# Moving the start addresses of the matmul operands in the MLP of a hybrid encoder block

## The chip, the core and the metric

The kernel runs on one core of a Trainium2 chip. The metric is device time in microseconds (us) for one execution. In the profile PE is the engine that multiplies matrices and PEld is its weight load; DVE, ACT and POOL are the vector, scalar and GpSimd engines, and SP issues most of the DMA transfers.

## The reference, cut to what matters

One layer (SEQ = 512 tokens, D_MODEL = 1024, D_FF = 2816) is attention in three head groups with an output projection, then a gated MLP with a causal convolution of width 3, then a gated per-layer input. The change touches the storage of the MLP's operands and of all weights that are split in two:

```python
def conv_gated_mlp(h, w_up, conv_w, conv_b, w_down):
    u = h @ w_up
    ...
    gate, val = jnp.split(c, 2, axis=-1)
    return (jax.nn.silu(gate) * val) @ w_down
...
h = h + conv_gated_mlp(rms_norm(h, ln_ffn[i]), w_up[i], conv_w[i], conv_b[i], w_down[i])
gate = jax.nn.sigmoid(rms_norm(h, ln_ple[i]) @ w_ple_gate[i])
h = h + (p[i] @ w_ple_proj[i]) * gate
```

## The kernel before

Every operand of a product is held as two float32r tiles, a high part and a low part: ACT copies the value into the high tile, DVE subtracts the high part from the value and writes the low tile (`split`, L207). Each product of two such operands is three matmuls (`mm3`, L223), and a matmul here always loads 128x128 stationary values (an LDWEIGHTS in the profile) and streams a moving operand of 256, 384 or 512 columns past them.

The parts that matter are these.

- **Wide products of the MLP** (`up_plain`, L1232, tile `u` in the profile): the stationary operand is a 128x128 part of a weight tile (`w_hi`, `w_lo`), the moving operand is one row block of the normed activations, `Th` or `Tl`, 512 columns. They are 960 matmuls.
- **Narrow products of the MLP**, 256 columns. One group is the up-projection by seven products in place of eight (`up_seven`, tiles `sX`, `sY`, `sZ`), whose moving operand is half a row block of `Th`/`Tl`, or a block of the sums `xh`/`xl`. The other is the down-projection, also by seven products (`Down.product`, tiles `dn_X`, `dn_Y`, `dn_Z`), whose moving operand is a block of a left tile (`g_ah`, `g_al`; for the last phase `xh`, `xl`). They are 1092 matmuls: 924 in the down-projection and 168 in the up-projection. `part` (L1089) cuts a weight tile into its 128-column parts.
- **Gate of the per-layer input** (tile `pg`): moving `Th`/`Tl`, stationary for the first four output blocks a weight tile (`w_hi`, `w_lo`), for the last four a left tile (`wg_ah`, `wg_al`, or the rest of `xh`, `xl`). The last block is done in two halves of 256 columns. **Projection of the per-layer input** (tile `pp`): moving a left tile (`pT_ah`, `pT_al`), 512 columns.
- **Projections of the attention** (`A_z`, `B_z`, `C_z` and their variants): here the activations `Th`/`Tl` are stationary and the split weights move. In the output projection (`wo`) the weights are stationary again.

All split weights go through one ring of tiles with the tags `whi` and `wlo`, 8 buffers each. The order of the MLP's work is set by a planner at the end of the function, which uses fixed costs per kind of work (a matmul group costs `n * 0.1177` us, L1043) and knows nothing of addresses; SP, POOL and the other engines get the order that it writes out. POOL adds weights in DRAM by accumulating transfers, one at a time (`add_sums`, L1168).

**Where the operands start.** What a matmul reads is a stretch of every one of 128 partitions, so an operand has one start address in bytes. Taken modulo 512, the program's allocation gives before the change:

- `Th`, `Tl`: 128. Every block starts at a multiple of 1024 bytes further on.
- weight tiles (`w_hi`, `w_lo`, 768 floats = 3072 bytes = 6 x 512): 128, and every 128-column part (512 bytes) the same.
- left tiles (`g_ah`, `g_al`, `pT_ah`, `wg_ah`, 7168 bytes = 14 x 512) and `xh`, `xl`: 320, and every block of 1024 bytes the same.

Below a pair such as (320, 128) means: moving operand at 320, stationary operand at 128, both modulo 512.

Of the kernel before, what the change touches and what calls it, by code (L numbers as in the profile page):

```python
# [8 lines left out]
F32 = mybir.dt.float32  # L9
F32R = mybir.dt.float32r  # L10
# [5 lines left out]
P = 128  # L16
D = 1024
S = 512
# [60 lines left out]
def kernel(ctx: ExitStack, tc: tile.TileContext, x, xt0, xt, pt_in, small, bias_c,  # L79
# [9 lines left out]
    nc = tc.nc  # L89
# [56 lines left out]


    pi = ctx.enter_context(tc.tile_pool(name="pi", bufs=1))
    W = {"pool": pi, "n": 768, "raw": 4, "hi": 8, "lo": 8}

    def load_w(src_fn, nk, m, n, name, eng=dve, gain=None, later=False):

        wp, we = W["pool"], W["n"]
        raw = wp.tile([P, we], F32, tag="wraw", bufs=W["raw"], name=f"{name}_r")
        for dst, src in src_fn(raw):
            dma = sp.dma_start(out=dst, in_=src)
            if later:
                tc.keep_in_program_order(dma)
        hi = wp.tile([P, we], F32R, tag="whi", bufs=W["hi"], name=f"{name}_h")
        lo = wp.tile([P, we], F32R, tag="wlo", bufs=W["lo"], name=f"{name}_l")  # L160
        hv, lv = (t[:, : nk * n].rearrange("p (k c) -> p k c", k=nk) for t in (hi, lo))
        rv = raw[:, : nk * m].rearrange("p (k c) -> p k c", k=nk)
        if later:
            def split():
                act.copy(hv[:, :, :m], rv)
                eng.tensor_tensor(out=lv[:, :, :m], in0=rv, in1=f32(hv[:, :, :m]), op=ALU.subtract)
                return hv, lv

            return split
        if eng == "dma":  # L170

            act.copy(hv[:, :, :m], rv)
            act.activation(lv[:, :, :m], rv, AF.Copy, scale=-1.0)
            nc.gpsimd.dma_start(out=lv[:, :, :m], in_=rv, accum_op=ALU.add)
            return hv, lv
        if gain is not None and eng is nc.gpsimd:
            for k in range(nk):
                eng.tensor_scalar(rv[:, k], rv[:, k], gain[:, k : k + 1], 1.0, ALU.mult, ALU.mult)
        if gain is None or eng is nc.gpsimd:
            act.copy(hv[:, :, :m], rv)  # L180
            eng.tensor_tensor(out=lv[:, :, :m], in0=rv, in1=f32(hv[:, :, :m]), op=ALU.subtract)
        else:
            for k in range(nk):
                hk, lk, rk = (v[:, k, :m] for v in (hv, lv, rv))
                act.activation(hk, rk, AF.Copy, scale=gain[:, k : k + 1])
                dve.scalar_tensor_tensor(lk, rk, gain[:, k : k + 1], f32(hk), ALU.mult, ALU.subtract)
        return hv, lv


    NRAW, NHI = 6, 7  # L190
    RING = {"raw": [], "hi": [], "lo": []}

    def in_turn(what, n):
        ring = RING[what]
        if len(ring) < n:
            tag = what
            if what == "raw" and len(ring) >= W["raw"]:
                tag = ("hi", "lo")[(len(ring) - W["raw"]) % 2]
            ring.append(pi.tile([P, 768], F32 if what == "raw" else F32R, tag=f"w{tag}", bufs=W[tag], name=f"w_{what}{len(ring)}"))
        else:  # L200
            ring.append(ring[-n])
        return ring[-1]
# [1 line left out]
    def raw_tile():  # L204
        return in_turn("raw", NRAW)

    def split(t, n, gain=None, to=None, eng=dve):  # L207

        hi, lo = to or [in_turn(q, NHI)[:, :n] for q in ("hi", "lo")]
        if gain is None:  # L210
            act.copy(hi, t[:, :n])
            eng.tensor_tensor(out=lo, in0=t[:, :n], in1=f32(hi), op=ALU.subtract)
        else:
            act.activation(hi, t[:, :n], AF.Copy, scale=gain)
            dve.scalar_tensor_tensor(lo, t[:, :n], gain, f32(hi), ALU.mult, ALU.subtract)
        return hi, lo
# [95 lines left out]
    def first_products():  # L312
        for k in range(KD):
            n = 384
            if k % 2 == 0:
                wh, wl = (pi.tile([P, 768], F32R, tag=f"w{q}", bufs=W[q], name=f"A0_{k // 2}_{q}") for q in ("hi", "lo"))
            a = slice((k % 2) * n, (k % 2 + 1) * n)
            th, tl = Th[k // 4][:, k % 4, :], Tl[k // 4][:, k % 4, :]
            g = h[:, 3, 0:1] if k == 0 else col(C_MIX, k)
            if k == 0:  # L320
                for c in (slice(0, H), slice(H, S)):
                    dve.tensor_scalar(th[:, c], XB[k][:, c], g, 1.0, ALU.mult, ALU.mult)
            elif k == 3:
                dve.tensor_scalar(th, XB[k], g, 1.0, ALU.mult, ALU.mult)
            else:
                act.activation(th, XB[k], AF.Copy, scale=g)
            act.copy(wh[:, a], WA[k])
            dve.tensor_tensor(out=wl[:, a], in0=WA[k], in1=f32(wh[:, a]), op=ALU.subtract)
            dve.scalar_tensor_tensor(tl, XB[k], g, f32(th), ALU.mult, ALU.subtract)
            for i, (ta, w) in enumerate(((Th, wh), (Th, wl), (Tl, wh))):  # L330
                for t in range(NT):
                    pe.matmul(z0[t][:, :n], tcol(ta, k, t), w[:, a], start=k == 0 and i == 0, stop=k == KD - 1 and i == 2)
            if k == 1:
                load_x(3)
        ws = [w() for w in first_b]
        for t in range(NT):
            stats(t)
        ev = [in_unit("A0", 0, 384, t, None, []) for t in range(NT)]

        rs = [ev[t][0](rest=False) for t in range(2)]  # L340
        for t in range(NT):
            ev[t][1](rs[t])
            if t < 2:
                rs.append(ev[t + 2][0](rest=False))
        for t in range(NT):
            ev[t][0](sums=False)
        return ws
# [723 lines left out]
                self.tiles = [q.rearrange("p j c -> p (j c)") for q in left_tiles(self.name)]  # L1071
            return [q[:, i * S : i * S + n] for q in self.tiles]

    def split_of(w, deps=(), gain=None, group=None, i=0):

        w.hi_slot = Slot("hi") if group is None else group.slot
        makes = [w.hi_slot] if not w.hi_slot.users else []

        def do():
            w.hi, w.lo = split(w.t, w.n, gain, None if group is None else group.get(i, w.n))  # L1080

        w.split = Task("do", [AC(w.n), DV(w.n * (1 if gain is None else 1.12))], do, (w.load, *deps), makes, [w.raw] + ([] if makes else [w.hi_slot]))
        return w
# [20 lines left out]
    def seven_weights(f):  # L1104

        size = (768, 768, 768, 768, 512)
        usum = USUM[f].rearrange("p i c -> p (i c)")
        ws = [tile_of(n, f"ws{f}_{i}", w_up[f][:, 768 * i : 768 * i + n] if i < 2 else usum[:, 768 * (i - 2) : 768 * (i - 2) + n],
                      deps=SUM_TASKS.get(("u", f), ()) if i > 1 else ()) for i, n in enumerate(size)]
        for w in ws:  # L1110
            split_of(w)
        order = (0, 1, 4, 3, 6, 5, 2)
        at_ = lambda j, i: part(ws[(4 * order[j] + i) // 6], (4 * order[j] + i) % 6)
        need_ = lambda j: [ws[q] for q in sorted({(4 * order[j] + i) // 6 for i in range(4)})]
        return at_, need_

    def down_weights(ph, n, name, tag="raw"):

        m = w_down[ph].shape[4]
        src = {f"{c + 1}{'eo'[i]}": w_down[ph][n, i, c] for i in range(2) for c in range(2)}  # L1120
        src.update({what: DSUM[ph][:, i, n] for i, what in enumerate(("S2", "S1", "1e2e", "1oS2"))})
        return lambda what: split_of(tile_of(m, f"{name}_{what}", src[what], tag, SUM_TASKS.get(("d", ph), ()) if "S" in what or "2e" in what else ()))

    def row_weights(src, name, gain=None, group=None, i=0):
        return split_of(tile_of(S, name, src), LAST_X if isinstance(group, Rest) else (), gain, group, i)
# [417 lines left out]
    def square3(j):  # L1543

        s = Slot("conv")
        sq_slots.append(s)
        first = j == 0

        def do():
            if first:  # L1550
                pin = mp.tile([P, D + 40], F32, tag="pin", bufs=1, name="sums3")
                v3["sums"], v3["rb"] = pin[:, :S], pin[:, S:D]
            v3[j] = v3["sums"] if first else mtmp(F32, 1, f"n3_sq{j}")
            act.activation(v3[j], hj(j), AF.Square)

        def add():
            (dve if j >= 6 else pool).tensor_tensor(out=v3["sums"], in0=v3["sums"], in1=v3[j], op=ALU.add)

        deps = [H_ADDS[j // 4, q] for q, p in PRODUCTS.items() if p[4] == j // 2 % 2]
        if first:  # L1560
            v3["last"] = Task("do", [AC(S)], do, deps, [sum_slot])
        else:
            a = Task("do", [AC(S)], do, deps, [s])
            v3["last"] = Task("do", [DV(S) if j >= 6 else ("pool", 1.35)], add, [a, v3["last"]], (), [s, sum_slot])
# [94 lines left out]
    t = 0.0  # L1659
# [122 lines left out]
```

## Time and profile before

| what | value |
|---|---|
| runs before | 708.51 us median of 3 (707.37 to 709.40) |
| the profiled execution, its own time | 709.23 us |
| its span, first to last instruction | 707.5 us |
| granted TensorE clock, mean | 0.999 |
| PE busy in the span | 691.2 us (98%) |
| DVE / ACT / POOL busy | 546.5 / 393.9 / 224.3 us |

Reading it: matmuls on PE are pipelined, and the profile gives each a duration from its start until its result is out. The 280 ns of a matmul with 256 columns and the 389 ns of one with 512 are such durations, and neighbours overlap. What a matmul costs in a stretch without idle time is the distance from its start to the next one's start. The chain of waits gives this directly, since it counts each piece only up to the start of the next: a piece "2.12 PE dn_X x18" is 18 matmuls at 117.8 ns.

### The profile page before, as it was taken

The page shows a single profiled execution, that of the slowest core. Times are in us where ns is not written, and L with a number is a line of the kernel's source. Part 1 is how long each engine was busy: PE and PEld are TensorE (multiplying, and loading weights), DVE is VectorE, ACT ScalarE, POOL GpSimd, SP SyncE. Part 2 cuts the span into 40 slices and gives each one's busy share as a digit, 9 for nine tenths or more (in the row PEclk, how much of TensorE's full clock was granted, in tenths as well). Part 3 has the DMA queues.
Part 4 walks back from the last instruction along what each step waited for, and adds up shares of the span by engine and source line. Part 5 has one row for each costly group of instructions (what it writes and reads, how often), then busy time and mean ns, then how long its engine had stood idle before and what let it go on. Part 6 is the DMA issues. An engine that isn't in the chain of part 4 may idle for free.

```text
span 707.5 us, 11539 instructions
## 1 busy us (share of the span) xinstructions
PE 691.2 (98%) x4028; PEld 618.6 (87%) x4028; DVE 546.5 (77%) x1110; ACT 393.9 (56%) x737; POOL 224.3 (32%) x324
## 2 busy tenths in 40 slices
PE   9988999999999999999999999999999999999997
PEld 8988989988999988868888899988988888999786
DVE  7678787887878874788877874798776787788764
ACT  6646766766666762566454543554444555546831
POOL 5676776757665440420111011001101110001310
PEclk9999999999999999999999999999999999999999
DMA  9454658746335313453686887878887774652531
GB/s 328 179 149 118 195 176 231 222 148 209 98 119 180 124 41 119 139 183 111 167 184 127 229 200 186 187 144 233 234 201 148 146 201 109 216 171 81 175 112 68
DMA packets 48471, 116.52 MB, mean 165 GB/s; under 512 B 5494, under 2 KB 7158, under 8 KB 48412
## 3 DMA queue, kind: packets, MB, share of 16 engines
q1 hardware_dynamic: 40476, 96.59, 42.0%
q0 software_dynamic: 7648, 18.88, 16.9%
q8 instruction: 32, 0.52, 0.3%
q10 hardware_dynamic: 288, 0.30, 0.1%
q14 instruction: 27, 0.22, 0.1%
HBM read 108.53 MB, written 31.47 MB: 198 GB/s over the span
## 4 chain that ended last, share of the span: by engine, by line
PE 78%; DVE 7%; DMA 6%; ACT 4%; POOL 2%; issue 2%; SPq 0%; ACTq 0%; POOLq 0%; DVEq 0%
PE u L105 30%; PE dn_X L105 9%; PE C_z L105 6%; PE pg L105 6%; PE wo L105 5%; PE dn_Y L105 4%; PE B_z L105 4%; PE dn_Z L105 2%; DMA bias_B<-fk_d 1%; DMA h<-in_x_dram 1%; PE sX L105 1%; DMA waq<-in_w_in_dram 1%; PE C_s L105 1%; PE C_po L105 1%; PE B_s L105 1%
## 5 line engine op out<-in xcount | busy, mean ns | idle before, releaser
L105 PE MATMUL u<-Tl,w_hi 128*128 128x512 f32 x320 | 124.9, 390 | 0.4 <-DVE Tl L105 0.4
L105 PE MATMUL u<-Th,w_hi 128*128 128x512 f32 x320 | 124.6, 389 | 0.0
L105 PE MATMUL u<-Th,w_lo 128*128 128x512 f32 x320 | 124.6, 389 | 0.0
L105 ACT CAST w_hi<-w_raw 128x768 fp32r<-128x768 f32 (+1 forms) x116 | 88.3, 784 | 62.1 <-PE dn_X L105 20.3
L105 DVE TENSOR_TENSOR w_lo<-w_raw,w_hi 128x768 fp32r<-128x768 f32 (+1 forms) x114 | 101.4, 909 | 17.4 <-ACT w_hi L105 16.5
L105 DVE SCALAR_TENSOR_TENSOR c<-u,cols,c 128x511 f32<-128x511 f32 x80 | 59.5, 746 | 22.2 <-ACT c L105 21.1
L105 PEld LDWEIGHTS u<-Tl,w_hi 128*128 128x128 f32 x320 | 60.1, 188 | 13.3 <-DVE Tl L105 1.3
L105 PEld LDWEIGHTS u<-Th,w_lo 128*128 128x128 f32 x320 | 60.1, 188 | 12.5 <-POOL w_lo L105 0.2
L105 PEld LDWEIGHTS u<-Th,w_hi 128*128 128x128 f32 x320 | 60.1, 188 | 12.5 <-ACT Th L105 0.4
L105 ACT ACTIVATE c<-u,cols 128x512 f32<-128x512 f32 x40 | 31.1, 778 | 25.3 <-PE u L105 25.1
L105 POOL DMA_DIRECT2D dsum<-in_w_dadd_dram x16 | 13.1, 821 | 89.7 <-DMA dsum<-in_w_dadd_dram 72.5
L105 PE MATMUL dn_X<-g_ah,w_hi 128*128 128x256 f32 x144 | 40.3, 280 | 0.0
L105 PE MATMUL dn_X<-g_al,w_hi 128*128 128x256 f32 x144 | 40.3, 280 | 0.0
L105 PE MATMUL dn_X<-g_ah,w_lo 128*128 128x256 f32 x144 | 40.3, 280 | 0.0
L105 POOL DMA_DIRECT2D dsum<-dsum x16 | 13.0, 812 | 85.4 <-DMA dsum<-dsum 57.5
L105 PE MATMUL B_z<-B_h,Th 128*128 128x384 f32 x96 | 34.4, 358 | 0.8 <-DVE B_zn L105 0.6
L105 PE MATMUL C_z<-C_h,Th 128*128 128x384 f32 x96 | 34.2, 356 | 0.0
L105 PE MATMUL B_z<-B_h,Tl 128*128 128x384 f32 x96 | 32.3, 337 | 0.0
L105 PE MATMUL C_z<-C_h,Tl 128*128 128x384 f32 x96 | 32.3, 337 | 0.0
L105 PE MATMUL C_z<-C_l,Th 128*128 128x384 f32 x96 | 32.2, 336 | 0.0
L105 PE MATMUL B_z<-B_l,Th 128*128 128x384 f32 x96 | 32.2, 336 | 0.0
L105 DVE TENSOR_TENSOR h<-h,dn_X 128x512 f32<-128x512 f32 x24 | 16.4, 685 | 14.5 <-PE dn_X L105 14.5
(506 smaller groups left out, 2089.3 us busy)
## 6 DMA issues: line engine op xcount, KB each, us to landing
w_raw<-in_w_up_dram SPq DMA_DIRECT2D x44, 384.0 KB, 5.1
dsum<-in_w_dsum_dram SPq DMA_DIRECT2D x12, 768.0 KB, 6.8
w_raw<-dsum SPq DMA_DIRECT2D x24, 384.0 KB, 4.3
w_raw<-in_w_down_dram SPq DMA_DIRECT2D x18, 384.0 KB, 4.8
w_raw<-in_w_up_dram SPq DMA_DIRECT2D x20, 256.0 KB, 5.0
B_r<-in_w_in_dram SPq DMA_DIRECT2D x12, 384.0 KB, 3.8
C_r<-in_w_in_dram SPq DMA_DIRECT2D x12, 384.0 KB, 4.9
dsum<-in_w_dadd_dram POOLq DMA_DIRECT2D x12, 384.0 KB, 6.6
```

Source lines behind the costliest of these rows:

```text
L105: ins = getattr(self.eng, op)(*a, **k)
```

## The change

The program's instructions stay the same ones in the same order on PE, ACT, DVE, POOL and SP; what differs is where tiles lie.

- Weight tiles become 64 floats longer (`ROOM`): 3328 bytes = 6.5 x 512. Consecutive buffers so start in turn at 128 and at 384 modulo 512.
- The weights of the narrow products (those of `up_seven` and of the down-projection) are written 16 floats = 64 bytes into their tile (`NARROW`, the new argument `c0`), so at 192 or 448. The wide ones stay at the tile's start, 128 or 384.
- The tile `pin` of the norm before the gate takes 48 floats more. The MLP's pool ends at a fixed address, so this puts the whole pool 192 bytes lower: left tiles, `xh` and `xl` start at 128.
- The scratch for descriptors of dynamic transfers at address 0 shrinks from 16384 to 8192 bytes per partition. Everything that lies behind it up to the weight tiles moves down by 8192 bytes, which changes nothing modulo 512.

| operand, start modulo 512 | before | after |
|---|---|---|
| `Th`, `Tl` | 128 | 128 |
| left tiles, `xh`, `xl` | 320 | 128 |
| weights of wide products, of the attention's projections | 128 | 128 or 384 |
| weights of narrow MLP products | 128 | 192 or 448 |

```diff
     pi = ctx.enter_context(tc.tile_pool(name="pi", bufs=1))
+    ROOM, NARROW = 64, 16
...
-        hi = wp.tile([P, we], F32R, tag="whi", bufs=W["hi"], name=f"{name}_h")
-        lo = wp.tile([P, we], F32R, tag="wlo", bufs=W["lo"], name=f"{name}_l")
+        hi = wp.tile([P, we + ROOM], F32R, tag="whi", bufs=W["hi"], name=f"{name}_h")
+        lo = wp.tile([P, we + ROOM], F32R, tag="wlo", bufs=W["lo"], name=f"{name}_l")
...
-            ring.append(pi.tile([P, 768], F32 if what == "raw" else F32R, tag=f"w{tag}", bufs=W[tag], name=f"w_{what}{len(ring)}"))
+            ring.append(pi.tile([P, 768 if tag == "raw" else 768 + ROOM], F32 if what == "raw" else F32R, tag=f"w{tag}", bufs=W[tag], name=f"w_{what}{len(ring)}"))
...
-    def split(t, n, gain=None, to=None, eng=dve):
-
-        hi, lo = to or [in_turn(q, NHI)[:, :n] for q in ("hi", "lo")]
+    def split(t, n, gain=None, to=None, eng=dve, c0=0):
+
+        hi, lo = to or [in_turn(q, NHI)[:, c0 : c0 + n] for q in ("hi", "lo")]
...
-                wh, wl = (pi.tile([P, 768], F32R, tag=f"w{q}", bufs=W[q], name=f"A0_{k // 2}_{q}") for q in ("hi", "lo"))
+                wh, wl = (pi.tile([P, 768 + ROOM], F32R, tag=f"w{q}", bufs=W[q], name=f"A0_{k // 2}_{q}") for q in ("hi", "lo"))
...
-    def split_of(w, deps=(), gain=None, group=None, i=0):
+    def split_of(w, deps=(), gain=None, group=None, i=0, c0=0):
...
-            w.hi, w.lo = split(w.t, w.n, gain, None if group is None else group.get(i, w.n))
+            w.hi, w.lo = split(w.t, w.n, gain, None if group is None else group.get(i, w.n), c0=c0)
...
         for w in ws:
-            split_of(w)
+            split_of(w, c0=NARROW)
...
-        return lambda what: split_of(tile_of(m, f"{name}_{what}", src[what], tag, SUM_TASKS.get(("d", ph), ()) if "S" in what or "2e" in what else ()))
+        return lambda what: split_of(tile_of(m, f"{name}_{what}", src[what], tag, SUM_TASKS.get(("d", ph), ()) if "S" in what or "2e" in what else ()), c0=NARROW)
...
-                pin = mp.tile([P, D + 40], F32, tag="pin", bufs=1, name="sums3")
+                pin = mp.tile([P, D + 88], F32, tag="pin", bufs=1, name="sums3")
...
-    nc = _bacc.Bacc("TRN2", target_bir_lowering=False, num_devices=1)
+    nc = _bacc.Bacc("TRN2", target_bir_lowering=False, num_devices=1, dynamic_dma_scratch_size=8192)
```

## The prediction

> **What bounds the kernel now.** I read the page first, then the waits of PE, then the chain of waits, and only then the timeline, because the group rows give durations that overlap.
>
> ```profile
> span 707.5 us, 11539 instructions
> PE 691.2 (98%) x4028; PEld 618.6 (87%) x4028; DVE 546.5 (77%) x1110; ACT 393.9 (56%) x737; POOL 224.3 (32%) x324
> PE u L105 <- DVE Tl L105: 0.2, 1, 0.2
> PE pg L105 <- DVE Tl L105: 0.7, 1, 0.7
> ```
>
> The last two rows are all that PE waits for from 316 us to the end. From the first `u` to the last `dn` the MLP is one unbroken row of matmuls, so each nanosecond on the distance between two starts there is a nanosecond on the end. The change moves no instruction; it can act only on these distances. The chain of waits shows them, here from 395 to 456 us (start, us, what):
>
> ```profile
> 395.56 2.12 PE dn_X L105 x18
> 397.68 2.72 PE u L105 x12
> ...
> 432.16 1.43 PE sX L105 x12
> 433.59 2.82 PE sZ L105 x24
> 436.41 1.36 PE sY L105 x12
> 437.77 1.36 PE sX L105 x12
> 439.13 2.04 PE dn_X L105 x18
> 441.17 1.42 PE sY L105 x12
> 442.59 2.06 PE dn_Y L105 x18
> 444.65 2.04 PE dn_X L105 x18
> 446.69 1.36 PE sX L105 x12
> 448.05 2.04 PE dn_Z L105 x18
> 450.09 2.04 PE dn_X L105 x18
> 452.13 2.04 PE dn_Y L105 x18
> 454.17 2.04 PE dn_X L105 x18
> ...
> 488.87 2.12 PE dn_X L105 x18
> ```
>
> This is the central observation. Matmuls of one shape, 256 columns, run at three speeds:
>
> - 2.12/18 = 117.8 ns: moving a left block, pair (320, 128). So runs nearly all of the down-projection.
> - 2.04/18 = 1.36/12 = 113.3 ns: the same pair, between 436 and 456 us, entered behind products of another pair and left when wide products come.
> - 1.43/12 = 119 ns: moving `Th`/`Tl`, pair (128, 128); its settled distance is 120 ns, since such a train starts faster (42 matmuls of the attention with the same pair give 5.02/42 = 119.5).
>
> ```profile
> 73.60 5.02 PE A1b_z L105 x42
> ```
>
> The wide `u` at (128, 128) takes 2.72/12 = 226.7 ns, which is exactly twice 113.3. I read 113.3 per 256 columns as the speed of an undisturbed stream. Then `u` has nothing to gain, and the narrow products pay 4.4 or 6.7 ns each.
>
> Other pairs bear on what address does. From the timeline (start, duration, instruction):
>
> ```profile
> 296.92 0.39 PE L105 MATMUL pp<-pT_ah,w_hi 128*128 128x512 f32 x1
> 299.25 0.39 PE L105 MATMUL pp<-pT_al,w_hi 128*128 128x512 f32 x1
> 680.46 0.39 PE L105 MATMUL pg<-Th,wg_ah 128*128 128x512 f32 x1
> 685.27 0.39 PE L105 MATMUL pg<-Th,wg_ah 128*128 128x512 f32 x1
> 697.06 0.28 PE L105 MATMUL pg<-Tl,wg_ah 128*128 128x256 f32 x1
> 698.12 0.28 PE L105 MATMUL pg<-Tl,wg_ah 128*128 128x256 f32 x1
> ```
>
> Ten distances of `pp` make 2.33 us: 233 ns at (320, 128). Twenty-one of `pg` make 4.81: 229 ns at (128, 320). Nine of its narrow half make 1.06: 118 ns at (128, 320). So 512 columns cost 226.7, 229 or 233 ns, and 256 cost 113.3, 118 or 120, and the speed goes with the pair in every row, with one pair, (320, 128), that has two speeds for 256 columns.
>
> [...]
>
> **The change part by part.** The sum is made against the profiled execution, 709.23 us (span 707.5, 1.73 around it), which is 0.72 above the median of the runs, 708.51.
>
> *Narrow products.* Their number, from one of the three matmuls of each product:
>
> ```profile
> L105 PE MATMUL dn_X<-g_ah,w_hi 128*128 128x256 f32 x144 | 40.3, 280 | 0.0
> L105 PE MATMUL dn_Y<-g_ah,w_hi 128*128 128x256 f32 x72 | 20.2, 280 | 0.0
> L105 PE MATMUL dn_Z<-g_ah,w_hi 128*128 128x256 f32 x36 | 10.1, 280 | 0.0
> L105 PE MATMUL dn_X<-xh,w_hi 128*128 128x256 f32 x32 | 9.0, 281 | 0.0
> L105 PE MATMUL sX<-Th,w_hi 128*128 128x256 f32 x8 | 2.3, 282 | 0.0
> L105 PE MATMUL sX<-xh,w_hi 128*128 128x256 f32 x16 | 4.5, 278 | 0.0
> ```
>
> With `dn_Y` and `dn_Z` on `xh` at a half and a quarter of `dn_X`, and `sY`, `sZ` at 8 each, that is 3 x 308 = 924 matmuls of the down-projection, 3 x 32 = 96 of the up-projection on `xh`, and 3 x 24 = 72 on `Th`. The chain's stretch from 436 to 456 us already holds 162 of them at 113.3 (two trains there, `sY` and `dn_Y`, at 118.3 and 114.4, roughly cancel against the end of `sZ` before it). All now get the pair (128, 192) or (128, 448), which no row shows. Bounds: from below 113.3, the least that any row has and half of the wide 226.7; from above 120, the most. I take 113.3. The reason is the 20 us in which the left blocks hold that speed over nine trains: it is a state that can be had. It was seen with the weights 64 bytes past the moving operand modulo 256 (320 + 64 = 384 = 128 + 256), and both new pairs have that distance; what the change adds is that the moving operand now starts where that of the undisturbed wide products does. Gain: (924 + 96 - 162) x 4.45 = 3.82, and 72 x 6.7 = 0.48, together **-4.3 us**. At the upper bound: 858 x 2.2 + 162 x 6.7 = **+3.0 us**.
>
> *Wide products.* `u` keeps `Th`/`Tl` at 128; by the layout, of the loads during its 960 matmuls some 540 are at 384 now. No row shows (128, 384). Bounds: 226.7, if a shift of 256 changes nothing, and 233, the dearest wide row: 0 to 540 x 6.7 = 3.6 us; with some 130 more in `wo` and `pg`, 0 to 4.5. I take 0, because the two wide pairs that do cost something have their operands 192 apart, one way and the other, and (128, 384) is nearer to (128, 128) if distances of 256 count as none, as I took it for the narrow ones.
>
> *Gate.* 84 wide matmuls go from (128, 320) to (128, 128): 229 to 226.7, -0.2 us. The 48 narrow ones at the end go to (128, 128): 118 to 120, +0.1 us.
>
> *`pp`.* 48 matmuls could gain 6.7 ns, 0.3 us, but the chain runs beside them:
>
> ```profile
> 305.90 2.35 DVE rb_ah L105
> 308.27 0.76 DVE hn L105
> 309.06 0.63 ACT Th L105
> ```
>
> The norm on DVE and ACT covers them, so 0; without the cover -0.3.
>
> *Attention.* The split weights move there, half of them from 384 now against `Th` at 128. 384 columns at (128, 128) take 4.69/27 = 173.7 ns, against 170 for 1.5 times 113.3:
>
> ```profile
> 186.05 4.69 PE C_z L105 x27
> ```
>
> For the roughly 400 matmuls that start at 384 that is between -1.5 us (170) and +1.6 (177, the same distance up); I take 0, as for `u`.
>
> *Scratch.* The page and the list of DMA issues show
>
> ```profile
> q0 software_dynamic: 7648, 18.88, 16.9%
> POOL dsum L105 <- DMA dsum<-in_w_dadd_dram: 93.6, 16, 8.8
> ```
>
> The whole program sends 7648 packets through this queue over its 708 us, and POOL waits for each adding transfer before the next (16 waits of 93.6 us together for one kind), so that half the scratch still has few of them to hold at a time. I take 0. The other end is a POOL that waits longer, with its adds late and `w_raw<-dsum` behind them on SP's queue; the nearest row prices that at one adding transfer's wait, 93.6/16 = 5.9 us, more than the whole forecast gain once; I give it no chance of its own.
>
> *What becomes late when PE is faster.* In the stretch at 113.3 PE already ran without a wait, so weights, left tiles and accumulators keep up at that pace, and I add no new wait.
>
> Sum: -4.3 - 0.2 + 0.1 = -4.4: 704.8 for the profiled execution, **704.1 us** for a median.
>
> **The rivals.**
>
> 1. *The difference alone counts, modulo 256.* Old: 128 - 320 = -192, which is 64 modulo 256. New: 64. Then the left blocks stay where they were, mostly 117.8; only the 72 on `Th` gain 2.2 each (-0.2), and the lucky stretch may be lost (162 x 4.45 = +0.7). 708.3 to 709.2, say **708.5**. For it: the pair (320, 128) has the good state and does not keep it. Against: it leaves unexplained why that state is left so easily.
> 2. *The address is not the cause.* The speed follows from how far the weight load lags at a train's entry, and address only goes with it by chance. Nothing changes: **708.5**. For it: two speeds at one pair. Against: 960 `u` of one speed, and each other pair with its own. [...]
> 3. *Moving from 128 is what makes 120.* The long narrow trains that move from 128 past weights at 128 are the slowest. Then a shift of the weights by 64 bytes does not free them, each of the 858 pays 2.2 more and the 162 pay 6.7: +3.0 us, **711.5**. It decides as soon as the new distance is above about 117.2, the mean now. For it: the 120 of `sX<-Th` and `A1b_z`. Against: `pg` at (128, 320) takes 118.
> 4. *The wide weights at 384 cost.* 670 matmuls x 2.3 (as `pg`) = +1.5, or x 6.7 (as `pp`) = +4.5. With the narrow gain: 705.6 to 708.6; without it 710 to 713. **708** in the middle.
>
> **How the numbers follow.** Forecast 0.47; rival 1 0.14; rival 2 0.06; rival 3 0.13; rival 4 0.20. About 0.3% (2.1 us) is what a measurement tells from no change: faster is below 706.4, slower above 710.6. Faster: 0.47 and 0.08 of rival 4, 0.55. Same: rivals 1 and 2, 0.20, less a little that strays. Slower: rival 3 and the rest of 4, 0.25. The likeliest case's own range is 702.6 (attention at its lower bound) to 706. The range for 8 in 10 is **702.6 to 711.5**, which leaves out half of rival 3 and the dear end of rival 4.
>
> **What would show it.** In the chain, down-projection pieces of 18 at 2.04 and of 30 at 3.40, `sX` pieces of 12 at 1.36 also on `Th`; `u` pieces of 12 still 2.72; 21 `pg` on `wg_ah` 4.76. A `dn` piece of 2.12 speaks for rivals 1 and 2, of 2.16 for 3; a `u` piece of 2.75 or 2.80 for 4. PE's waits from 316 us on should stay under 1 us; if they grow, the gain was given back to DVE or a transfer, and the forecast fails for a reason I have not priced.

## The result

| | before | after |
|---|---|---|
| runs side by side, median | 708.68 us (707.37 to 709.93, 11 runs) | 710.03 us (707.91 to 712.52, 11 runs) |
| ratio after / before | | 1.0014, 95% interval 1.0003 to 1.0026 |
| profiled execution, its own time | 709.23 us | 710.33 us |
| its span | 707.5 us | 708.6 us |

The change brought no gain: the measurement puts it 0.2 to 1.8 us above the kernel before, which is inside the 0.3% that the prediction called no change. The page of the profile after begins with its span and the busy time of each engine:

```profile
span 708.6 us, 11539 instructions
PE 692.6 (98%) x4028; PEld 620.3 (88%) x4028; DVE 546.5 (77%) x1110; ACT 394.2 (56%) x737; POOL 224.0 (32%) x324
```

Its waits of PE from the first `u` on are the two of before (total, times, longest):

```profile
PE pg L105 <- DVE Tl L105: 0.7, 1, 0.7
PE u L105 <- DVE Tl L105: 0.2, 1, 0.2
```

PE is 1.4 us busier with the same 4028 matmuls and waits as long as before. So the question is only what distance from start to start the matmuls have. The chain of waits of the kernel after, in the stretch that the prediction quoted of the kernel before (start, us, what):

```profile
316.98 78.95 PE u L105 x347
395.93 2.12 PE dn_X L105 x18
398.05 2.75 PE u L105 x12
...
432.63 1.41 PE sX L105 x12
434.05 2.83 PE sZ L105 x24
436.88 1.41 PE sY L105 x12
438.29 1.41 PE sX L105 x12
439.70 2.12 PE dn_X L105 x18
441.82 1.41 PE sY L105 x12
443.24 2.12 PE dn_Y L105 x18
...
455.25 2.12 PE dn_X L105 x18
```

Every narrow train is at 2.12/18 = 117.8 ns; the pieces of 12 at 1.41 have the same mean in the trace. The stretch from 436 to 456 us, which ran at 113.3 ns before, is gone, and nothing else has got that speed. The trains on `Th` went from 1.43 to 1.41.

For all narrow products together I took, from the trace, the distance from each matmul's start to the next one's start on PE and summed it over the 1092 matmuls (this number is called the **narrow sum** below): 128.00 us before, 128.61 after. The 0.61 is, to rounding, the lost stretch, 0.74 (0.54 in the down-projection, 0.20 in the sevens on the sums), less the gain of the 72 on `Th`, 0.12. The wide `u` of this stretch add 0.2: pieces of 12 behind a down-projection take 2.75 in place of 2.72, while a long one keeps 50.34/222 = 226.8 ns:

```profile
558.28 50.34 PE u L105 x222
```

Other `u` run ahead of the chain's first long piece of them, and other `pg` ahead of the one that waits for `Tl`; the chain goes through other engines there. From that first long piece of `u` to the `pg` that waits, the kernel before has in its chain

```profile
316.64 78.92 PE u L105 x347
661.94 4.14 PE pg L105 x17
666.94 35.83 PE pg L105 x180
```

and the kernel after, whose piece of 347 `u` stands above,

```profile
663.13 4.15 PE pg L105 x17
668.13 35.73 PE pg L105 x180
```

So the kernel before took 661.94 - 316.64 = 345.30 us for it, the kernel after 663.13 - 316.98 = 346.15. That is +0.85, where the sums give 0.61 + 0.2. What lies ahead of it, 0.3 us more in this profile, is no more than one execution differs from the next: in a second profile of the kernel before the down product behind this piece starts 0.8 us later than in the first, at 396.39 against 395.56.

The gate's 180 matmuls took 35.83 before and 35.73 now. In the timeline of the kernel after (start, duration, instruction) 21 of them on `wg_ah` are 4.76 us apart, 226.7 ns each where it was 229, and 18 of the narrow half 2.16 us, 120 ns where it was 118:

```profile
681.61 0.39 PE L105 MATMUL pg<-Th,wg_ah 128*128 128x512 f32 x1
686.37 0.39 PE L105 MATMUL pg<-Th,wg_ah 128*128 128x512 f32 x1
698.05 0.28 PE L105 MATMUL pg<-Tl,wg_ah 128*128 128x256 f32 x1
700.21 0.28 PE L105 MATMUL pg<-Tl,wg_ah 128*128 128x256 f32 x1
```

### The profile page after: what moved, and what is told of

The parts are those of the page before. It is cut to its first block, busy times and chain, and to the rows that moved or that the text cites. A ratio compares the mean times of both kernels' runs of the same rounds, so it can differ in the third digit from the quotient of the medians.

```text
span 708.6 us, 11539 instructions
## 1 busy us (share of the span) xinstructions
PE 692.6 (98%) x4028; PEld 620.3 (88%) x4028; DVE 546.5 (77%) x1110; ACT 394.2 (56%) x737; POOL 224.0 (32%) x324
## 4 chain that ended last, share of the span: by engine, by line
PE 80%; DVE 8%; DMA 4%; ACT 4%; POOL 2%; issue 2%; SPq 0%; ACTq 0%; POOLq 0%; DVEq 0%
PE u L105 30%; PE dn_X L105 9%; PE C_z L105 6%; PE pg L105 6%; PE wo L105 5%; PE dn_Y L105 4%; PE B_z L105 4%; PE dn_Z L105 2%; DMA bias_B<-fk_d 1%; PE A1b_z L105 1%; PE sX L105 1%; DMA h<-in_x_dram 1%; PE C_s L105 1%; PE A_z L105 1%; PE C_po L105 1%
## 5 line engine op out<-in xcount | busy, mean ns | idle before, releaser
L105 ACT CAST w_hi<-w_raw 128x768 fp32r<-128x768 f32 (+1 forms) x116 | 88.2, 783 | 62.6 <-PE dn_X L105 19.7
L105 POOL TENSOR_TENSOR sums<-sums,n_sq 128x512 f32<-128x512 f32 x5 | 6.9, 1375 | 70.6 <-ACT n_sq L105 70.5
```

Of the source, the lines that this page charges most:

```text
L105: ins = getattr(self.eng, op)(*a, **k)
```

## The experiments

"Distance" means here: start of the weights that are loaded, less start of the moving operand that streams meanwhile, modulo 256 bytes. Before, the left blocks have distance 64 (320 to 128) and the sevens on `Th` 0; after, all narrow products have 64 (128 to 192 or 448). Every speed is a mean distance from start to start over all matmuls of a group, from the trace. For the first eight runs only one execution each was timed; the 11 executions of before lie 2.6 us apart, so these runs are read by the narrow sum and the speeds.

### Does the speed follow the address?

Two runs give each group of the down-projection another shift of its weights, and put the same distances on other groups in the second run. The moving operand stays at 128.

```diff
+    DN_C0, SEVEN_C0 = {(0, 0): 0, (0, 1): 8, (1, 0): 32, (1, 1): 48, (2, 0): 24, (2, 1): 56}, 32
...
-            split_of(w, c0=NARROW)
+            split_of(w, c0=SEVEN_C0)
...
-        return lambda what: split_of(tile_of(m, f"{name}_{what}", src[what], tag, ...), c0=NARROW)
+        return lambda what: split_of(tile_of(m, f"{name}_{what}", src[what], tag, ...), c0=DN_C0[min(ph, 2), n])
```

> Edit of the changed kernel: the weights of each group of the down-projection start at a distance of their own past the moving operand, modulo 256 bytes: phase 0 half 0: 0, phase 0 half 1: 32, phase 1 half 0: 128, phase 1 half 1: 192, the last two phases 96 and 224; the seven products of the up-projection 128. Theory A (the distance modulo 256 and the state in which a train is entered set the speed): 0 gives 120.0 ns from start to start, 192 gives 117.8 as pg at (128, 320) did; 128, the farthest from a meeting of the two streams, 113.3; 32, 96 and 224 lie between. Theory B (the absolute address of the moving operand sets it): all groups 117.8, since all move from 128. Theory C (the address is not the cause): all 117.8, with no order by distance.

The second has `{(0, 0): 32, (0, 1): 48, (1, 0): 0, (1, 1): 40, (2, 0): 4, (2, 1): 60}, 48`.

> The same with the distances dealt out otherwise, so that place and distance are told apart: phase 0 half 0: 128, half 1: 192, phase 1 half 0: 0, half 1: 160, the last two phases 16 and 240; the seven products 192. Theory A: the speeds follow the distances of the first sweep to their new places (0: 120.0, 192: 117.8, 128: the same as there); 16 and 240 near 120. Theories B and C: 117.8 in every group, or speeds that stay with the place.

Two more runs filled in further distances, one moving from 128 and one from 320 (its `pin` as before):

> Moving from 128; distances modulo 256 by group: 208, 216, 232, 48, 80, 144; the seven products 224. In the first sweep 224 gave 116.7 and 192 gave 117.8. Theory A: a smooth valley near 216 to 224 at or under 116.7, and 48 and 80 between 117.8 and 118.3; 144 near 120. If 113.3 is to be had from a distance alone, one of these shows it through a whole group.

> The left tiles and xh, xl back at 320; distances modulo 256 by group: 224, 192, 0, 112, 48, 32; the seven products 224 on xh, xl and 160 on Th, Tl. Theory A with the distance alone: each as in the sweeps that moved from 128 (224: 116.7, 192: 117.8, 0: 120.0, 48 and 32 near 118). Theory B (the absolute address counts as well, as 118.7 against 120.0 at distance 128 hints): they differ by more than 1 ns from those.

Measured, ns from start to start, mean over the 126 or 210 matmuls of each group of the down-projection (at 128 from 320 over all 924, from the next run below):

| distance | moving from 128 | moving from 320 |
|---|---|---|
| 0 | 119.8, 119.9 | 119.9 |
| 16 / 32 | 118.3 / 118.2 | - / 118.3 |
| 48 | 122.5 | 117.9 |
| 64 (after; before) | 117.8 | 117.8 and 113.3 |
| 80 / 96 | 118.7 / 118.3 | - |
| 112 | - | 120.0 |
| 128 | 120.1, 120.3 | 118.6 |
| 144 / 160 | 119.4 / 119.8 | - |
| 192 | 117.8, 117.8 | 117.8 |
| 208 / 216 | 116.7 / 119.6 | - |
| 224 | 116.7 | 116.8 |
| 232 / 240 | 118.4 / 119.9 | - |

Pieces of these runs' chains show it directly. The first run, where 128 and 192 follow each other within 15 us:

```profile
497.57 2.16 PE dn_Z L105 x18
512.57 2.12 PE dn_Z L105 x18
```

The run that moves from 128 with finer steps, at 208 and then at 48:

```profile
414.80 2.10 PE dn_Z L105 x18
510.51 2.22 PE dn_Z L105 x18
```

A group takes the speed of its distance wherever it stands in the program: 192 moved from the second group of phase 1 to the second of phase 0 and kept 117.8, and 0 moved from the first group of phase 0 to the first of phase 1. So the address is the cause (rival 2 falls). The curve is not smooth: 208 and 224 are the best means, with 216 between them 3 ns dearer, and 128, from which the first run's expectation hoped for 113.3, is among the slowest. All four narrow sums and times are above those of before, though not in one order: 129.47, 130.02, 129.71 and 129.25 us, times 712.01, 710.91, 710.12 and 711.73 beside 708.71 (first two) and 709.34 of before. None reached 113.3.

The distance is not the whole cause, and some means hide two speeds. At 144, in the run of finer steps, the first two products (36 matmuls) run at 116.7 ns and the later ones at 120.0:

```profile
616.66 2.10 PE dn_Y L105 x18
640.15 3.60 PE dn_X L105 x30
```

At 48 from 128 the products behind other narrow ones run at 123.3 (the 2.22 above), the one behind wide products at 118.4; from 320 those behind wide products take 118.3. So what a train comes from counts at these distances too.

### Undoing one part

Left tiles back at 320, the weights' shift kept, so that the left blocks have distance 128 and the sevens on `Th` 64:

```diff
-                pin = mp.tile([P, D + 88], F32, tag="pin", bufs=1, name="sums3")
+                pin = mp.tile([P, D + 40], F32, tag="pin", bufs=1, name="sums3")
```

> The changed kernel with the left tiles and xh, xl back at 320 (pin as before), the weights of narrow products still 64 bytes further: distance 128 modulo 256 on the left blocks, 64 on Th and Tl. Theory A: the left blocks show what distance 128 shows in the sweeps, Th and Tl 117.8. Theory B: moving from 320 as before, 117.8 with a stretch of 113.3. Theory C: 117.8.

Down products at 118.6, sevens on the sums at 119.2, on `Th` at 116.9; narrow sum 129.48, 710.11 us beside 708.71. The shift of the weights without that of the left tiles is dearer than both together, and the left tiles' alone would make distance 0, at 119.9 in the table: the difference of the two starts counts for most of it. It is not all: distance 128 gives 118.6 from 320 and 120.1 to 120.3 from 128.

The mean of the sevens on `Th` hides something that bears on the prediction. One train of them, `sY`, comes right behind down products that run at 120 ns from 320:

```profile
438.77 2.16 PE dn_X L105 x18
440.93 1.38 PE sY L105 x12
```

It takes 115.0 ns on the mean: its first matmuls up to 122 ns, all from the fourth on 113 or 114. They stand at (128, 448), one of the pairs of the change. So that pair has the fast speed; the sevens on `Th` that begin behind wide products take 117.8 in this run.

The longer tiles and the small scratch alone, with no shift and the left tiles at 320:

```diff
-    ROOM, NARROW = 64, 16
+    ROOM, NARROW = 64, 0
...
-                pin = mp.tile([P, D + 88], F32, tag="pin", bufs=1, name="sums3")
+                pin = mp.tile([P, D + 40], F32, tag="pin", bufs=1, name="sums3")
```

> The longer tiles and the smaller scratch alone: weights at 128 or 384, left tiles and xh, xl at 320, no 64 bytes of extra distance. Distances modulo 256 are then those of the kernel before. Theory A: every group as before, wide 226.7, left blocks 117.8, Th and Tl 120.0, and total within 1 us of before. If a distance of 256 counted, half the tiles would change speed.

Narrow sum 128.00, `u` at 226.8 as in before, the stretch at 113.3 intact, 709.53 us beside 709.34. A start 256 bytes further, the longer tiles and the scratch are worth nothing, either way.

### Is the stretch at 113.3 chance?

The kernel before once more, as it stands:

> The kernel before, unchanged, profiled a second time. Theory A (distance modulo 256, and a state that the entry fixes): the stretch at 113.3 ns from 436 to 456 us is there again, since the program and so the entry are the same. Theory D (the stretch is chance, a matter of how two streams happen to lie in time): it is missing, shorter, or at another place.

```profile
437.24 1.36 PE sY L105 x12
438.60 1.36 PE sX L105 x12
439.96 2.04 PE dn_X L105 x18
...
455.00 2.04 PE dn_X L105 x18
457.04 13.16 PE u L105 x58
```

The same trains have it, to the piece, and the narrow sum is again 128.00. (It took 710.18 us beside 709.34, so one time says little.) The speed of 113.3 ns is no chance: it is reached at the same place of the order in both profiles, and in that of the longer tiles. Ahead of it stand the sevens on `Th` at (128, 128), which run at 120 ns. A first guess was that leaving any 120 ns train is enough. So in the kernel after the sevens were put at distance 0:

```diff
-            split_of(w, c0=NARROW)
+            split_of(w)
```

> The changed kernel with the weights of the up-projection's seven products at their tile's start (distance 0 modulo 256), those of the down-projection still at 64. Theory A: the seven products at 120.0; the down-projection's trains that follow them without a wide product between run at 113.3 until the next wide product, as before the change, and all others at 117.8. Theory B: seven products 120, all of the down-projection 117.8. Theory C: all 117.8.

```profile
435.88 1.44 PE sY L105 x12
437.32 1.44 PE sX L105 x12
438.75 2.12 PE dn_X L105 x18
440.88 1.44 PE sY L105 x12
442.31 2.12 PE dn_Y L105 x18
```

The sevens run at 119.8 and the down products right behind them stay at 117.8; narrow sum 128.95, 709.62 us. The guess failed. The difference from the kernel before that stands out: there the *moving* operand changes its place between the two trains (128 to 320), here the weights do.

### What leads into the 113.3 ns

First, an entry by the weights again, now at the layout of before with the longer weight tiles: the first down product of each run of two or more behind wide ones gets its weights 192 bytes further (distance 0), the rest none.

```diff
+        ... c0=48 if (ph, n, what) in ENTRY else 0)
```

> Layout of before for the left blocks (moving from 320), weights in the longer tiles at 128 or 384, so nearly all narrow products have distance 64 modulo 256 as before. One thing is new: the first down product of each run of two or more after wide products has its weights 192 bytes further in, at distance 0 (pair (320, 64) or (320, 320)), which costs 119.9 ns a matmul in e8. Theory 'the 113.3 ns state is entered from a train of 120 ns': all that follow such a first product run at 113.3 until the next wide one; about 700 of 1020 matmuls gain 4.4 ns, the first ones lose 2: narrow sum about 125.1 us (before 128.0), total about 2.9 us under before. Rival 'it needs the jump of the moving operand from 128 to 320, as between the products on Th and on the left blocks': the rest stays at 117.8, narrow sum 128.2 to 128.8 and total 0.1 to 0.8 above before.

The first products cost 119.4, the rest stayed at 117.2 on the mean with the one old stretch; narrow sum 128.08, ratio 0.9995 (0.9984 to 1.0006). The theory of a 120 ns train ahead failed again, and its rival, the jump of the moving operand, is what the next run tries.

Then an entry by the moving operand. Block 0 of each left tile starts at 128 or 384, the other blocks 192 bytes further, at 320 or 64 (the left tiles are longer now, so that they alternate too), and `xh`, `xl` at 320. All weights stand at 128 or 384, so modulo 256 block 0 has distance 0 and the rest 64.

```diff
+    class Left:
+        def __init__(self, t):
+            self.first, self.rest = t[:, :H], t[:, H + 48 : 7 * H + 48].rearrange("p (j c) -> p j c", c=H)
...
-        return tuple(mp.tile([P, 7, H], F32R, ...) for tag in ("ah", "al"))
+        return tuple(Left(mp.tile([P, 7 * H + 64], F32R, ...)) for tag in ("ah", "al"))
```

> Longer weight tiles, no shift of the narrow weights (128 or 384). The left tiles keep block 0 at 128 modulo 512 and have all further blocks and xh/xl 192 bytes further, at 320: so the first product of each group of seven runs at (128, 128), distance 0, about 120 ns, and the others at distance 64, entered from a train of 120 ns with a jump of the moving operand from 128 to 320, as in the stretch of before at 113.3 ns. Theory 'the jump of the moving operand makes the entry': the others run at 113.3 until wide products come, narrow sum about 125.5 us, total about 2.4 us under before. Rival 'the entry depends on more than the pair ahead (length of the train ahead, or how far the weight loads have run ahead)': the others stay at 117.8 and block 0 at 120, narrow sum 128.2 to 128.6, total 0.2 to 0.6 above before.

The chain of this kernel behind a long wide train (`dn_X` at 488.42 is on block 0):

```profile
469.83 18.59 PE u L105 x82
488.42 2.15 PE dn_X L105 x18
490.57 2.06 PE dn_Y L105 x18
492.63 2.04 PE dn_X L105 x18
494.67 2.04 PE dn_Z L105 x18
...
515.19 2.73 PE u L105 x12
517.93 2.12 PE dn_X L105 x18
...
637.07 3.40 PE dn_X L105 x30
```

Block 0 pays 119 ns, and behind it the products run at 113.3 until wide ones come; the single product behind those is at 117.8 again. The narrow sum is 125.74 us, 2.26 less than before (expected 125.5).

Does this hold for the pairs of the change, whose 113.3 the prediction took? In the kernel after, block 0 was laid behind the other six and 64 bytes further, at 192 or 448; the rest lies at 128 or 384, with the weights at 192 or 448:

```diff
+            self.first, self.rest = t[:, 6 * H + 16 : 7 * H + 16], t[:, : 6 * H].rearrange("p (j c) -> p j c", c=H)
```

> The kernel after, with one block moved: block 0 of each left tile lies behind the other six and starts 64 bytes further, at 192 or 448 modulo 512, so the first product of each group of seven has distance 0 to its weights (192 or 448) and runs near 120 ns; the next product's moving operand jumps back to 128 while its weights stay where they are. That is the same jump by 64 bytes modulo 256 as in e10, but it leads to the pairs of the change, (128, 192) and (128, 448), whose 113.3 the prediction took and which the profile after never shows. Theory 'every pair at distance 64 has both states, and a jump of the moving operand out of a 120 ns train leads to 113.3': the down products behind each such first product run at 113.3 until wide ones come, narrow sum near 126 us against 128.6 of the kernel after, total about 2.5 us under after and 2 under before. Rival 'the fast state belongs to operands at 320': they stay at 117.8, narrow sum 128.8, total 0.2 above after.

```profile
489.80 2.15 PE dn_X L105 x18
491.95 2.06 PE dn_Y L105 x18
494.01 2.04 PE dn_X L105 x18
```

It does. Narrow sum 125.71; the down products other than block 0's at 114.1 on the mean, against 117.8 after. 708.19 us median (10 runs) beside 709.22 of before, ratio 0.9982 (0.9969 to 0.9994).

Last, the gap behind block 0 alone, all weights at 128 in tiles as short as before; the small scratch stays and pays for the gap's space:

```diff
-    ROOM, NARROW = 64, 0
+    ROOM, NARROW = 0, 0
```

> As e10, with the weight tiles as short as before, so that all weights start at 128 modulo 512 and only the gap of 192 bytes behind block 0 of the left tiles (and the small scratch, which pays for its space) is left of the edits. Theory, from e10's records: narrow sum near 125.7 us against 128.0 before, the last phase at 113.3; 2.3 us on the path, ratio about 0.997. Rival 'e10's gain needs weights alternating between 128 and 384': narrow sum 128.2 or more, ratio 1.000.

| | narrow sum | median | ratio to before, 95% |
|---|---|---|---|
| before | 128.00 | 709.22 | |
| after | 128.61 | 710.03 (beside 708.68) | 1.0003 to 1.0026 |
| gap, long weight tiles | 125.74 | 708.09 (beside 709.09) | 0.9972 to 1.0004 |
| gap in the kernel after | 125.71 | 708.19 | 0.9969 to 0.9994 |
| gap alone | 125.74 | 708.36 | 0.9971 to 0.9996 |

The three kernels with a gap agree in the narrow sum and lie 0.9 to 1.0 us below before by their medians. Less arrives than the 2.26 us saved. In the chain of the last kernel, over the same stretch from `u` to `pg`:

```profile
318.33 78.95 PE u L105 x347
661.99 3.01 PE pg L105 x12
```

That is 343.66 us, 1.64 less than before's 345.30. The rest is given back at the end of the down-projection, where PE now waits longer for the norm:

```profile
PE pg L105 <- DVE Tl L105: 1.3, 1, 1.3
```

It was 0.7. This profiled execution was a late one ahead of the stretch (318.33 against 316.64) and took 709.23 us like that of before, so the gain has to be read from the medians: two of the three intervals lie below 1, one reaches past it. A gain of about 1 us over before is at the edge of what the runs resolve; the speeds of the trains are not.

## Why the prediction was wrong

The forecast was 704.1 us; the median is 710.03. Of the rivals, the first (the difference alone counts, modulo 256) came nearest in its mechanism: nothing gained on the left blocks, the fast stretch lost. Its time, 708.3 to 709.2 us, still lies under the median. From the traces its kind of loss is 0.85 us, against 1.35 between the medians; the interval, 0.2 to 1.8, takes in both. And the difference alone does not decide: at one distance two speeds stand, as the prediction held against it.

- **Narrow products, the step that failed.** "All now get the pair (128, 192) or (128, 448), which no row shows ... I take 113.3 ... it is a state that can be had." Measured 117.8 on all of them: the term of -4.3 us was +0.6. That the state can be had is true, also at these pairs (the gap in the kernel after has it, and one train with the left tiles back at 320). That a better start of the moving operand would hold the trains in it was not: at distance 64 the runs show two states, and which one a train got went with how it was entered. Trains behind wide products got 117.8; those behind a 120 ns train whose moving operand started elsewhere got 113.3. The prediction had both facts in its rows, two speeds at one pair and a stretch "entered behind products of another pair", and still took the speed as a property of the pair. The change leaves the distance at 64, and behind wide products the speed stayed at 117.8; and it puts the left blocks where `Th` is and the sevens on `Th` at 117.8, which takes away both the 120 ns train and the jump of the moving operand behind it that made the fast stretch. Bringing back the 120 ns train alone did not restore it (117.8); bringing back both did.
- **The lost stretch.** Rival 1 had it as +0.7; measured +0.74. It is the main part of the loss in the narrow sum.
- **Sevens on `Th`.** Forecast -6.7 ns each, rival 1 -2.2; measured 119.4 to 117.8, -1.6.
- **Wide products.** Taken at 0; measured 226.7 to 226.8 in long trains before, at (128, 128), and after, at (128, 128) and (128, 384) in turn, and +0.2 us in the entries behind narrow trains. Right, and the reasoning that a distance of 256 counts as none was right (rival 4 falls).
- **Gate.** -0.2 and +0.1, as forecast: 226.7 for 229, 120 for 118.
- **`pp`.** Forecast to change behind its cover. Ten distances are 2.26 us now, 226 ns where it was 233 (rows below, from the timeline of the kernel after), and the chain's piece of 347 `u` still starts 19.7 us behind the first of them, 316.98 - 297.27 against 316.64 - 296.92. Right.

```profile
297.27 0.39 PE L105 MATMUL pp<-pT_ah,w_hi 128*128 128x512 f32 x1
299.53 0.39 PE L105 MATMUL pp<-pT_al,w_hi 128*128 128x512 f32 x1
```

- **Attention.** Taken at 0, half of the moving weights at 384. The piece of 27 `C_z` takes 4.69 us in the chains before and after alike. Right.
- **Scratch, waits of PE.** Nothing, as forecast: PE waits 0.9 us in all from the first `u` on, before and after, and POOL's 16 waits for one kind of adding transfer (`dsum<-in_w_dadd_dram`) are 93.6 us before and 91.1 after.
- **Rival 2, the address is not the cause**: it named the same 708.5 us as rival 1, for the wrong reason. The sweeps show the speed going with the address; that the entry counts as well, which was the argument for it, is true. That a lag of the weight load at the entry sets the speed was not shown. The time of these float32r matmuls of 256 columns does depend on where their weights lie: with the moving operand kept at 128 and the weights shifted alone, the groups take from 116.7 to 122.5 ns.
- **Rival 3, moving from 128 makes 120**: falls. From 128 the means run from 116.7 to 122.5, and single trains reach 113.3. Of six distances tried from 128 and from 320 apart from 64, four (0, 32, 192, 224) have the same mean from both within 0.2 ns; 48 and 128 have not. At 48 the entry may explain it, since behind wide products it is 118.4 and 118.3; at 128, behind wide products, it is 120.5 from 128 and 118.4 from 320, so there the start itself, and not only the difference, seems to count.

What stays open: why a jump of the moving operand out of a 120 ns train leads into 113.3 ns and a jump of the weights to the same distance does not, and why wide products led into it in none of the profiles (at distance 64 the trains right behind them ran at 117.8). The runs show the first at four layouts (before, the left tiles back at 320, and the gap in both kernels) and the second at two; the mechanism inside PE was not observed.

## What to carry to other kernels

When one pair of addresses shows two speeds (here 117.8 and 113.3 ns), the pair is not the whole state: look at what stood ahead of the train before pricing a move. Work out what a change leaves the same (here the difference of the two starts) before what it alters. And a stretch that runs fast by accident is part of the baseline; an even layout can remove it (here 113.3 ns became 117.8).

## What the hardware showed unexpectedly

- A matmul of 256 columns in float32r took from 113.3 to 122.5 ns from start to start on the mean of a group, depending on where its operands lie and what ran ahead, with distances 8 bytes apart differing by 3 ns (208 and 216 bytes: 116.7 and 119.6). With 512 columns it took 226.7 at distance 0, 229 at 192 and 233 at 64.
- Trains kept their speed: at the same distance the same products ran at 117.8 or at 113.3 ns for 25 us and more, and 12 wide matmuls were enough to lose the better one. Two speeds at one distance were also seen at 144 (116.7 and 120.0) and at 48 (118.4 and 123.3).
- A difference of 256 bytes was none: 384 in place of 128 changed no speed in long trains of the some 540 wide matmuls that have it (50.32 us before and 50.34 after for the piece of 222), and none of the narrow ones (narrow sum 128.00 both ways).
